# A two-layer mixer on one core: the identity and small constants move behind all other pools in SBUF

## The chip, the core and the metric

The kernel runs on one core of a Trainium2 chip. The metric is the device time of one execution in microseconds (us). TensorE is called PE in the profile, its weight loads PEld, VectorE DVE, ScalarE ACT, GpSimd POOL and SyncE SP.

## What is computed

Two layers of a mixer over 512 positions with 1024 features, all in float32. Each layer, cut to what matters:

```
xn = rmsnorm(x, pre_g);  proj = xn @ w_in
y_a = gated MLP of 128-position blocks (layernorm, lower-triangular w_s) * silu(z_a)
y_b = 8-head latent attention (low-rank q and kv, a shared rotary key) * silu(z_b)
y_c = 8-head attention over chunks of 64 with a learned bias * silu(z_c)
merged = sum over i of sigmoid(xn @ w_gate_i + gate_b_i) * (y_i @ w_branch_i)
x = x + rmsnorm(merged @ w_out, post_g)
```

## The kernel before

Each float32 matmul is done in three. An operand is split into a high part in `float32r` and a low part, the rest (`x - high`, also in `float32r`), and `mm3` adds high x high, high x low and low x high (lines 113, 114, 115) into one PSUM tile. In `t_.matmul(out, lhsT, rhs)`, `rhs` is the moving operand, which streams through the array column by column, and `lhsT` the stationary one, which is loaded ahead of it. In a row of the profile the moving operand stands first: `pm<-A_h,whi` moves `A_h` past `whi`.

Weights come in pieces of 128 x 1024 (4096 bytes in each of the 128 partitions) by DMA into `wraw`, of which there are three buffers. ACT casts a piece to `whi`, and DVE or POOL subtracts to get `wlo` (lines 102 and 107). Of `whi` and `wlo` there are four buffers each. Two helpers use them:

- `fm_unit` (features by positions): the weights are stationary, and the normalised input, `A_h` and `A_l`, moves, 512 columns at a time, 24 matmuls in a unit. `gate_units` calls it for the 24 gate pieces of a layer and then does 12 matmuls with a branch's result moving: `ybh` and `ybl` for branch b, parts of the tile `X` for branches a and c.
- `tm_unit` (positions by features): `A_h` and `A_l` are stationary and `whi` and `wlo` move, 24 matmuls in a unit. The last unit of layer 2 is done in two halves of 256 columns.

Attention adds scores (`ps_s`, with `qa`, `qb`, `ka`, `kl`, `qr`, `krs`, all from a ring of twelve tiles called `qk`, but `krs`, which is in `bk`), transposes of the softmax (`turn_p`: 128-wide matmuls with `ident` moving, `pt<-ident,pp`) and `av` (`po`, with `PT_h` and `PT_l` moving and `vt` stationary). A list `units` and a table `RATES` of credits set by hand how the units are mixed between the 128 softmax blocks of a layer's two attentions (64 a layer). The scheduler keeps that order.

Tiles lie in SBUF in the order in which pools are opened and, in a pool, in which tiles are made; each begins at the next multiple of 32 bytes in the partition. `cst` is the first pool and begins at byte 16512, a multiple of 128. It holds `ident`, 128 float32 (512 bytes), then `mhalf`, one float32, and then the large tiles, whose sizes are all multiples of 128 bytes; behind these come `col` (172 bytes) and `gbh` (96 bytes) of each layer, and then the pools `wp` (`wraw`, `whi`, `wlo`), `wk` and `sm`. So in the built program:

| tile | first byte before | modulo 128 | first byte after | modulo 128 |
|---|---|---|---|---|
| `ident` | 16512 | 0 | 228096 | 0 |
| `A_h` | 17056 | 32 | 16512 | 0 |
| `A_l`, `mrg`, `YT`, `X`, `vt`, `PT_h`, `PT_l` | 33440 to 113824 | 32 | 32896 to 113280 | 0 |
| `wraw`, `whi`, `wlo` (first of each) | 121056, 133344, 149728 | 96 | 119936, 132224, 148608 | 0 |
| `tmp`, `zs`, `ybh`, `ybl`, `bk`, `qk`, `pp`, `yo` | 166112 to 226528 | 96 | 164992 to 225408 | 0 |
| `ss`, `rs`, `bn`, `st`, `sso` (a few elements each) | 228576 and up | 0 to 96 | 227456 and up | 0 to 96 |

Parts of these tiles that matmuls use begin at multiples of 64 columns, 256 bytes, from there.

Of the kernel before, what the change touches and what calls it, by code (L numbers as in the profile page):

```python
# [8 lines left out]
F32 = mybir.dt.float32  # L9
# [6 lines left out]
P = 128  # L16
# [3 lines left out]
KT = D // P  # L20
# [3 lines left out]
H = 8  # L24
# [16 lines left out]
def trunk_kernel(ctx, tc, x, wtm, wqd, wrv, wqk, wfm, wgate, wbr, wout,  # L41
                 cols, post_g, ln_g, ln_b, sgu_wt, rel, csnd, out):
    nc = tc.nc
    v_, s_, g_, t_ = nc.vector, nc.scalar, nc.gpsimd, nc.tensor

    cst = ctx.enter_context(tc.tile_pool(name="cst", bufs=1))
    wp = ctx.enter_context(tc.tile_pool(name="wp", bufs=4))
    wk = ctx.enter_context(tc.tile_pool(name="wk", bufs=1))
    sm = ctx.enter_context(tc.tile_pool(name="sm", bufs=4))
    psm = ctx.enter_context(tc.tile_pool(name="psm", bufs=3, space=PSUM))  # L50
    pss = ctx.enter_context(tc.tile_pool(name="pss", bufs=2, space=PSUM))
    pst = ctx.enter_context(tc.tile_pool(name="pst", bufs=2, space=PSUM))
    pso = ctx.enter_context(tc.tile_pool(name="pso", bufs=1, space=PSUM))
    dr = ctx.enter_context(tc.tile_pool(name="dr", bufs=1, space=bass.MemoryType.DRAM))

    ident = cst.tile([P, P], F32, name="ident")
    make_identity(nc, ident)
    mhalf = cst.tile([P, 1], F32, name="mhalf")
    g_.memset(mhalf, -0.5)

    A_h = cst.tile([P, KT, S], F32R, name="A_h")
    A_l = cst.tile([P, KT, S], F32R, name="A_l")
# [10 lines left out]
    PT_h = cst.tile([P, TB * PTS + P], F32R, name="PT_h")  # L73
    PT_l = cst.tile([P, TB * PTS + P], F32R, name="PT_l")
    x1 = dr.tile([S, D], F32, name="x1")


    ZB = 3 * PTS + 2 * P
# [66 lines left out]
    def bk_t(n):  # L145
        return wk.tile([P, n], F32, name="bk", tag="bk", bufs=2)
# [28 lines left out]
        return i  # L175

    def load_consts(l):
        t = cst.tile([P, 4 * KT + H + 3], F32, name=f"col_{l}")
        nc.sync.dma_start(out=t, in_=cols[l])
        c = {"pre": t[:, 0:KT], "gb": t[:, KT:4 * KT], "sb": t[:, 4 * KT:4 * KT + H], "mg": t[:, 4 * KT + H:]}  # L180
        c["gbh"] = cst.tile([P, 3 * KT], F32, name=f"gbh_{l}")
        g_.tensor_scalar(out=c["gbh"], in0=c["gb"], scalar1=0.5, scalar2=None, op0=ALU.mult)
        return c

# [401 lines left out]
    for tb in range(TB):  # L586
        for hf in range(2):
            nc.sync.dma_start(out=x_rows(tb)[:, hf, :], in_=x[tb * P:(tb + 1) * P, hf * 512:(hf + 1) * 512])
        if tb == 0:
            cl = [load_consts(0)]  # L590
            raws += [load_raw(wqd[0, j], 832) for j in range(2)]
        if tb == 1:
            raws.append(load_raw(wqd[0, 2], 832))
# [4 lines left out]
    for l in range(L):  # L598
        c = cl[l]
        qk, zc, zb, st = {}, {}, {}, {}  # L600
        ya, yc, yb = [], [], []
        if l == 0:
            dgen = mla_down(l, st, raws, first)
            del raws
            step(dgen)
            norm_x(2, c)
            norm_x(3, c)
            cl.append(load_consts(1))
        else:
            st = st1  # L610
# [44 lines left out]
        for i in range(NS + LAG + 1):  # L655
# [32 lines left out]
            while credit > 0 and units and units[0][0] <= i:  # L688
                t = next(units[0][1], None)
# [14 lines left out]
        for hf in range(2):  # L704
            t = bk_t(S)
# [117 lines left out]
```

## Time and profile before

| | |
|---|---|
| median of 3 runs | 1101.63 us (1100.35 to 1102.0) |
| the profiled execution | 1102.16 us, its span 1100.4 us |
| granted PE clock, mean | 0.997 of full speed |
| busy: PE, DVE, ACT, POOL | 1075.0, 645.7, 529.2, 234.1 us |
| matmuls | 5096 |

The span is the time from the first to the last instruction of the profiled execution; 1.8 us lie around it. Matmuls overlap, so a matmul's duration is longer than the distance from its start to that of the next one; a stream's pace is read from starts.

### The profile page before, as it was taken

The page shows a single profiled execution, that of the slowest core. Times are in us where ns is not written, and L with a number is a line of the kernel's source. Part 1 is how long each engine was busy: PE and PEld are TensorE (multiplying, and loading weights), DVE is VectorE, ACT ScalarE, POOL GpSimd, SP SyncE. Part 2 cuts the span into 40 slices and gives each one's busy share as a digit, 9 for nine tenths or more (in the row PEclk, how much of TensorE's full clock was granted, in tenths as well). Part 3 has the DMA queues.
Part 4 walks back from the last instruction along what each step waited for, and adds up shares of the span by engine and source line. Part 5 has one row for each costly group of instructions (what it writes and reads, how often), then busy time and mean ns, then how long its engine had stood idle before and what let it go on. Part 6 is the DMA issues. An engine that isn't in the chain of part 4 may idle for free.

```text
span 1100.4 us, 14199 instructions
## 1 busy us (share of the span) xinstructions
PE 1075.0 (98%) x5096; PEld 886.9 (81%) x5096; DVE 645.7 (59%) x1332; ACT 529.2 (48%) x1073; POOL 234.1 (21%) x249
## 2 busy tenths in 40 slices
PE   6999999999999999999999999999999999999997
PEld 4887878888888888888787787788888888888886
DVE  5674776666566654334577756675656665534443
ACT  6454576445454543224563644664544545432331
POOL 2310132221123231210033111331212323221000
PEclk9999999999999999999999999999999999999999
DMA  7231132223233223334342322212223232323342
GB/s 238 78 101 63 52 102 85 70 81 101 77 96 96 69 86 109 95 114 153 104 133 92 104 74 67 85 58 87 91 73 106 89 86 79 102 77 96 106 150 80
DMA packets 37703, 104.65 MB, mean 95 GB/s; under 512 B 5376, under 2 KB 6400, under 8 KB 37632
## 3 DMA queue, kind: packets, MB, share of 16 engines
q1 hardware_dynamic: 37632, 103.74, 30.3%
q8 instruction: 40, 0.66, 0.3%
q14 instruction: 31, 0.25, 0.1%
HBM read 99.53 MB, written 4.19 MB: 94 GB/s over the span
## 4 chain that ended last, share of the span: by engine, by line
PE 45%; ACT 2%; DVE 2%; issue 1%; POOL 1%; DMA 0%; POOLq 0%; DVEq 0%; ACTq 0%
PE pm L114 13%; PE pm L113 13%; PE pm L115 13%; PE pt L361 2%; PE po L379 1%; PE po L378 1%; DVE wlo L107 0%; PE ps_s L419 0%; PE ps_s L418 0%; PE ps_s L436 0%; PE ps_s L438 0%; PE ps_s L437 0%; POOL rs L136 0%; PE pt L167 0%; DMA wraw<-in_wtm_dram 0%
## 5 line engine op out<-in xcount | busy, mean ns | idle before, releaser
L102 ACT CAST whi<-wraw 128x1024 fp32r<-128x1024 f32 (+3 forms) x194 | 177.1, 914 | 263.2 <-PE pm L114 156.9
L113 PE MATMUL pm<-A_h,whi 128*128 128x512 f32 x640 | 259.9, 406 | 0.0
L114 PE MATMUL pm<-A_l,whi 128*128 128x512 f32 x640 | 252.8, 395 | 0.0
L115 PE MATMUL pm<-A_h,wlo 128*128 128x512 f32 x640 | 252.7, 395 | 0.0
L107 DVE TENSOR_TENSOR wlo<-wraw,whi 128x1024 fp32r<-128x1024 f32 (+3 forms) x130 | 152.0, 1172 | 113.2 <-ACT whi L102 109.7
L107 POOL TENSOR_TENSOR wlo<-wraw,whi 128x1024 fp32r<-128x1024 f32 (+1 forms) x64 | 116.2, 1815 | 379.7 <-ACT whi L102 311.7
L113 PE MATMUL pm<-whi,A_h 128*128 128x512 f32 (+2 forms) x456 | 177.9, 390 | 2.6 <-ACT A_h L172 2.6
L114 PE MATMUL pm<-wlo,A_h 128*128 128x512 f32 (+2 forms) x456 | 176.1, 387 | 1.1 <-DVE wlo L107 1.1
L115 PE MATMUL pm<-whi,A_l 128*128 128x512 f32 (+2 forms) x456 | 176.3, 387 | 0.4 <-DVE A_l L173 0.2
L115 PEld LDWEIGHTS pm<-A_h,wlo 128*128 128x128 f32 x640 | 120.1, 188 | 29.1
L114 PEld LDWEIGHTS pm<-A_l,whi 128*128 128x128 f32 x640 | 120.4, 188 | 25.2
L113 PEld LDWEIGHTS pm<-A_h,whi 128*128 128x128 f32 x640 | 120.2, 188 | 25.2
L113 PEld LDWEIGHTS pm<-whi,A_h 128*128 128x128 f32 x456 | 86.5, 190 | 20.2 <-ACT A_h L172 4.5
L115 PEld LDWEIGHTS pm<-whi,A_l 128*128 128x128 f32 x456 | 86.4, 189 | 17.4 <-DVE A_l L173 2.0
L114 PEld LDWEIGHTS pm<-wlo,A_h 128*128 128x128 f32 x456 | 86.5, 190 | 17.0 <-DVE wlo L107 2.2
L354 DVE TENSOR_SCALAR pp<-pp,st 128x128 f32<-128x128 f32 (+3 forms) x128 | 70.2, 549 | 3.6
L367 ACT CAST PT_h<-pt 128x128 fp32r<-128x128 f32 (+3 forms) x128 | 53.9, 423 | 32.1 <-PE pt L361 31.0
L423 DVE CUSTOM_DVE_ANT_0 pp<-ps_s,bk 128x128 f32<-128x128 f32 (+1 forms) x64 | 31.2, 487 | 60.4 <-PE ps_s L419 60.1
L368 DVE TENSOR_TENSOR PT_l<-pt,PT_h 128x128 fp32r<-128x128 f32 (+3 forms) x128 | 61.6, 481 | 6.5 <-ACT PT_h L367 6.1
L361 PE MATMUL pt<-ident,pp 128*128 128x128 f32 x320 | 55.9, 272 | 1.5 <-DVE X L212 1.5
L444 ACT ACTIVATE pp<-ps_s,st 128x128 f32<-128x128 f32 (+1 forms) x64 | 33.8, 528 | 43.4 <-DVE st L442 42.7
L426 ACT ACTIVATE pp<-pp,st 128x128 f32<-128x128 f32 (+1 forms) x64 | 36.0, 563 | 37.6 <-DVE st L425 36.9
(180 smaller groups left out, 1581.8 us busy)
## 6 DMA issues: line engine op xcount, KB each, us to landing
wraw<-in_wgate_dram SPq DMA_DIRECT2D x48, 512.0 KB, 3.6
wraw<-in_wtm_dram SPq DMA_DIRECT2D x32, 512.0 KB, 3.5
wraw<-in_wfm_dram SPq DMA_DIRECT2D x32, 512.0 KB, 3.6
wraw<-in_wbr_dram SPq DMA_DIRECT2D x48, 256.0 KB, 2.6
wraw<-in_wout_dram SPq DMA_DIRECT2D x16, 512.0 KB, 3.6
bk<-in_rel_dram SPq DMA_DIRECT2D x16, 256.0 KB, 2.7
wraw<-in_wqd_dram SPq DMA_DIRECT2D x8, 416.0 KB, 4.2
mrg<-in_x_dram SPq DMA_DIRECT2D x8, 256.0 KB, 6.9
```

Of the source, the lines that this page charges most:

```text
L102: s_.copy(out=hi[:, :cols], in_=raw[:, :cols])
L107: i = e.tensor_tensor(out=lo[:, :cols], in0=raw[:, :cols], in1=f32(hi[:, :cols]), op=ALU.subtract)
L113: t_.matmul(out=ps, lhsT=lh, rhs=rh, start=start, stop=False)
L114: t_.matmul(out=ps, lhsT=lh, rhs=rl, start=False, stop=False)
L115: t_.matmul(out=ps, lhsT=ll, rhs=rh, start=False, stop=stop)
L354: v_.tensor_scalar(out=pp[:, :n], in0=pp[:, :n], scalar1=rc, scalar2=None, op0=ALU.mult)
L361: t_.transpose(pt[:, kb * P:(kb + 1) * P], pp[:, kb * P:(kb + 1) * P], ident)
L367: s_.copy(out=dst(PT_h), in_=src)
L368: v_.tensor_tensor(out=dst(PT_l), in0=src, in1=f32(dst(PT_h)), op=ALU.subtract)
L423: v_.tensor_tensor_reduce(out=pp[:, :n], in0=ps[:, :n], in1=bias[:, S - n:S], scale=1.0, scalar=-3e38, op0=ALU.add, op1=ALU.max, accum_out=mx)
L426: s_.activation(out=pp[:, :n], in_=pp[:, :n], func=AF.Exp, bias=nm, accum_out=se)
L444: s_.activation(out=pp[:, :n], in_=ps[:, :n], func=AF.Exp, bias=nm, accum_out=se)
```

## The change

The four small kinds of tile get a pool of their own, `cs`, which is opened after the other SBUF pools and so lies behind them. `make_identity` and the `memset` of `mhalf` stand some lines further down, still ahead of all other instructions of the kernel.

```diff
     sm = ctx.enter_context(tc.tile_pool(name="sm", bufs=4))
+    cs = ctx.enter_context(tc.tile_pool(name="cs", bufs=1))
     psm = ctx.enter_context(tc.tile_pool(name="psm", bufs=3, space=PSUM))
...
-    ident = cst.tile([P, P], F32, name="ident")
-    make_identity(nc, ident)
-    mhalf = cst.tile([P, 1], F32, name="mhalf")
-    g_.memset(mhalf, -0.5)
 
     A_h = cst.tile([P, KT, S], F32R, name="A_h")
...
     x1 = dr.tile([S, D], F32, name="x1")
+    ident = cs.tile([P, P], F32, name="ident")
+    make_identity(nc, ident)
+    mhalf = cs.tile([P, 1], F32, name="mhalf")
+    g_.memset(mhalf, -0.5)
...
     def load_consts(l):
-        t = cst.tile([P, 4 * KT + H + 3], F32, name=f"col_{l}")
+        t = cs.tile([P, 4 * KT + H + 3], F32, name=f"col_{l}")
...
-        c["gbh"] = cst.tile([P, 3 * KT], F32, name=f"gbh_{l}")
+        c["gbh"] = cs.tile([P, 3 * KT], F32, name=f"gbh_{l}")
```

On every engine the instructions and their order are the same in both programs; only the numbers of buffers and lines in their names differ. As an example, POOL at the start of the program, where the moved lines issue their work (`-` before, `+` after):

```order
 L819 UNCONDITIONAL_BRANCH
 masks.py:197 MEMSET ident 128x128
-L59 MEMSET mhalf 128x1
+L75 MEMSET mhalf 128x1
 L79 MEMSET PT_h 128x128
 masks.py:199 ISA
 masks.py:199 AFFINE_SELECT ident<-ident 128x128
 L80 MEMSET PT_l 128x128
-L182 TENSOR_SCALAR gbh_103<-col_101 128x24
+L182 TENSOR_SCALAR gbh_106<-col_104 128x24
```

The `memset` of `mhalf` stands where it stood, with another line number, and `gbh` and `col` have other buffer numbers; nothing moved.

## Rows read from the trace of the kernel before

**Rows 1.** The page, its head and part 1: busy time by engine.

```profile
span 1100.4 us, 14199 instructions
...
PE 1075.0 (98%) x5096; PEld 886.9 (81%) x5096; DVE 645.7 (59%) x1332; ACT 529.2 (48%) x1073; POOL 234.1 (21%) x249
```

**Rows 2.** The page, part 2: granted clock in tenths, 40 slices.

```profile
PEclk9999999999999999999999999999999999999999
```

**Rows 3.** The page, part 4: the chain that ended last, by engine.

```profile
PE 45%; ACT 2%; DVE 2%; issue 1%; POOL 1%; DMA 0%; POOLq 0%; DVEq 0%; ACTq 0%
```

**Rows 4.** PE's waits, the three longest: us in total, times, longest.

```profile
PE pt L167 <- DVE tmp L164: 10.2, 5, 7.1
PE pm L113 <- ACT A_h L172: 2.6, 2, 2.4
PE pt L361 <- DVE X L212: 1.5, 2, 0.8
```

**Rows 5.** Groups by line and form: count, then busy us, mean ns, idle.

```profile
L113 PE MATMUL pm<-A_h,whi 128*128 128x512 f32 x640 | 259.9, 406 | 0.0
...
L113 PE MATMUL pm<-whi,A_h 128*128 128x512 f32 x376 | 149.2, 397 | 0.0
...
L113 PE MATMUL pm<-X,whi 128*128 128x512 f32 x128 | 51.2, 400 | 0.0
...
L113 PE MATMUL pm<-ybh,whi 128*128 128x512 f32 x88 | 36.1, 410 | 0.0
```

**Rows 6.** Timeline of PE, 982 to 1049.3: start us, duration us, instruction.

```profile
982.06 0.39 PE L115 MATMUL pm<-ybh,wlo 128*128 128x512 f32 x1
982.29 0.39 PE L113 MATMUL pm<-A_h,whi 128*128 128x512 f32 x1
...
1049.25 0.40 PE L115 MATMUL pm<-X,wlo 128*128 128x512 f32 x1
```

**Rows 7.** Timeline of PE, 1049.4 to 1088.4.

```profile
1049.49 0.40 PE L113 MATMUL pm<-whi,A_h 128*128 128x512 f32 x1
...
1076.32 0.50 PE L114 MATMUL pm<-wlo,A_h 128*128 128x512 f32 x1
1076.65 0.39 PE L115 MATMUL pm<-whi,A_l 128*128 128x512 f32 x1
...
1088.34 0.39 PE L115 MATMUL pm<-whi,A_l 128*128 128x512 f32 x1
```

**Rows 8.** Timeline of PE, 953.1 to 955.9.

```profile
953.12 0.40 PE L113 MATMUL pm<-ybh,whi 128*128 128x512 f32 x1
953.36 0.40 PE L114 MATMUL pm<-ybl,whi 128*128 128x512 f32 x1
...
953.82 0.39 PE L113 MATMUL pm<-ybh,whi 128*128 128x512 f32 x1
...
955.86 0.39 PE L418 MATMUL ps_s<-qb 128*128 128x512 f32 x1
```

**Rows 9.** Timeline of PE, 256 columns: 232.7 to 233.1, and 1088.5 to 1094.

```profile
232.70 0.28 PE L436 MATMUL ps_s<-ka,qa 128*128 128x256 f32 x1
...
233.06 0.38 PE L361 MATMUL pt<-ident,pp 128*128 128x128 f32 x2
...
1088.57 0.28 PE L113 MATMUL pm<-whi,A_h 128*128 128x256 f32 x1
...
1093.90 0.28 PE L115 MATMUL pm<-whi,A_l 128*128 128x256 f32 x1
```

**Rows 10.** Groups by form: ACT's cast of a transposed softmax, PSUM to SBUF.

```profile
L367 ACT CAST PT_h<-pt 128x512 fp32r<-128x512 f32 x32 | 18.7, 584 | 9.3 <-PE pt L361 9.2
...
L367 ACT CAST PT_h<-pt 128x128 fp32r<-128x128 f32 x32 | 8.5, 264 | 0.7
```

**Rows 11.** SP's waits, the longest; and the loads of gate weights, us to landing.

```profile
SPq L90 <- DVE wlo L107: 551.7, 100, 20.4
...
wraw<-in_wgate_dram SPq DMA_DIRECT2D x48, 512.0 KB, 3.6
```

## The prediction

> **What bounds the kernel now.** I read the page first. TensorE (PE) is busy for 1075.0 of the 1100.4 us span, DVE for 59% and ACT for 48% [rows 1]. [...] The chain that ended last is mostly PE, with 2% each for ACT and DVE [rows 3], and its lines are the three matmuls of `mm3`. Next come PE's own waits: the two longest groups are 10.2 and 2.6 us, and six more are at most 1.5 us each [rows 4], so under 22 us in all. The kernel is one long stream of matmuls, and its time is the number of matmuls times the distance between their starts.
>
> That distance is not the mean duration of the groups (390 to 410 ns [rows 5]), since matmuls overlap; it is read from starts. [...] In the stretch that ends layer 1's mixers, 288 matmuls start from 982.29 to 1049.25: 66.96 us over 287 spacings, 233.3 ns each [rows 6]. [...]
>
> **What the spacing depends on.** In a row's `out<-in` the moving operand stands first, the stationary one second.
> - `A_h`, `A_l` or `X` moving, `whi` or `wlo` stationary: 233.3 ns [rows 6].
> - `whi` or `wlo` moving, `A_h` or `A_l` stationary: from 1049.49 to 1076.32, 115 spacings of 233.3; after one hiccup (0.33 us), from 1076.65 to 1088.34, 51 spacings of 229.2, same names and shape [rows 7]. The streams can settle in more than one rhythm.
> - `ybh` or `ybl` moving, `whi` or `wlo` stationary: after three starts, nine spacings from 953.82 to 955.86, 226.7 ns each [rows 8].
>
> `X` and `ybh` go through the same line, with the same stationary tile and shape; what differs is where the moving tile begins. Modulo 128 bytes, `A_h`, `A_l`, `X`, `vt`, `PT_h` and `PT_l` begin at 32, and `whi`, `wlo`, `ybh`, `ybl` and the twelve `qk` tiles at 96. So the start address seems to matter, and the fastest rhythm, 226.7, is that of a pair where both operands have the same offset (96, 96). After the change every one of these tiles begins at 0: one offset for all, and one that this trace never shows for a 512-wide operand. `ident` is at 0 already, but only in 128-wide transposes.
>
> **The change, part by part.** It adds and removes no instruction, and each engine's order is the same but for names; POOL's `make_identity` and `memset` stand where they stood. What changes is addresses.
>
> *PE, 512 columns wide.* 640 x 3 with `A_h`/`A_l` moving and 128 x 3 with `X` [rows 5], and 64 with `PT_h`/`PT_l`: 2368 at offset 32. 376 x 3 and 88 x 3 [rows 5], and 104 in small groups: 1496 at offset 96. Now: 2368 at 233.3, and 1496 somewhere from 226.7 to 233.3 (I take 230, between the rhythms of [rows 7, 8]); mean 232.0 over 3864. [...] Between ends so far apart I take 226.7, the rhythm of the only long-running pair with equal offsets [rows 8]. That gives 2368 x 6.6 = 15.6 us and 1496 x 3.3 = 4.9 us. Against it: the rhythm has to be found again after each break by a score, transposing or `av` matmul. The `ybh` run took three spacings for it (953.12 to 953.82, 0.70 us against 0.68); by an estimate of 200 breaks (128 softmax blocks, whose scores and transposes often stand apart) at 4 spacings of 5 ns each, 4 us are given back. Sum: 16.5 us.
>
> *PE, narrower.* 256 columns take 113.4 ns at the end (47 spacings from 1088.57 to 1093.90) and 120 among the scores (three from 232.70 to 233.06) [rows 9]. The second pair has equal offsets (96, 96), the first different ones. So equal offsets need not be best for short runs; I take 0, with 432 x 6.6 = 2.9 us as the bound either way.
>
> *ACT and DVE.* From 128 to 512 columns ACT's cast grows from 264 to 584 ns, 0.83 ns a column [rows 10]. Whatever a read that starts elsewhere saves or costs lies under PE, which waits under 22 us for all engines, half of it for `tmp` at each layer's start [rows 4]. I take 0; for a gain the bound is those 22 us. For a loss, ACT and DVE could grow by a tenth (53 and 65 us of work) and still have a third of the span free; without that cover, `whi` and `wlo` would come late and PE would wait for them.
>
> *Loads.* A 512 KB load lands 3.6 us after its issue, while SP waits 551.7 us for DVE to give a `wraw` buffer back [rows 11]. Loads wait for buffers, not the reverse: 0 either way. If a load became late, `whi` on ACT would be late next, then PE.
>
> PE has few waits, so I let the gain through whole: 1102.16 (the profiled execution, 0.5 us above the median of the three runs) less 16.5 is 1085.7; **predicted 1086**.
>
> **The rivals.**
> 1. *Address doesn't matter to the stream at this granularity, or offset 0 has the same cost as 32 and 96.* For it: one pair shows two rhythms at one set of addresses [rows 7], so the rhythm may be a matter of phase. Against it: `ybh` and `X` differ in a start address alone, and the run turns to 233.3 at once where `A_h` takes over from `ybh` at 982.29 [rows 6]. Time: 1100 to 1104, within 0.2% of now. [...]
> [...]
> 3. *Slower: one offset for all puts every stream in the slow rhythm.* Place: the 1496 matmuls at offset 96 lose their 226.7 and 229.2. For it: 256-wide pairs with equal offsets take 120 against 113.4 [rows 9]. Against it: the best 512-wide rhythm is an equal pair. [...] It decides once the mean spacing is over 232.6, which is 0.2% of the time more than now.
>
> **How the numbers follow.** About 0.2%, 2.2 us, is what a measurement of this kernel can tell from no change. Forecast (spacings of 224 to 231, 1072 to 1097): 0.38. Rival 1: 0.22. Rival 2: 0.18. Rival 3: 0.22. Faster 0.56, same 0.22, slower 0.22. The range runs from 1045, which leaves out the far half of rival 2 (0.09), to 1109, which leaves out the part of rival 3 in which spacings go past 234 (0.07); the forecast's own range is 1072 to 1097.
>
> **What would show it.** In the profile after: the starts in the stretch of `A_h,whi` matmuls near 985 to 1045, about 226.7 apart if I am right, 233.3 by rivals 1 and 3, 220 or less by rival 2; the spacing in the last stretch of `whi,A_h` the same as in that of `ybh,whi`, if the offset decides. PE's busy time falls with its span, DVE's and ACT's do not. I am wrong if spacings fall but PE begins to wait for `whi`, `wlo` or softmax (the gain would then show as waits of PE), or if the rhythm depends on the order in which streams meet and not on addresses.

## The result: 1.5% faster, and the profile after

| | before | after |
|---|---|---|
| median | 1101.0 us (4 runs, 1100.35 to 1102.0) | 1084.49 us (4 runs, 1084.22 to 1085.1) |
| ratio, 95% interval | | 0.985 [0.9833, 0.9867] |
| the profiled execution, its span | 1102.16, 1100.4 us | 1084.56, 1082.8 us |

The page after, its head, part 1 and the granted clock of part 2, against [rows 1, 2]:

```profile
span 1082.8 us, 14199 instructions
...
PE 1057.6 (98%) x5096; PEld 885.7 (82%) x5096; DVE 645.8 (60%) x1332; ACT 529.7 (49%) x1073; POOL 234.2 (22%) x249
...
PEclk9999999999999999999999999999999999999999
```

PE is busy 17.4 us less and the span is 17.6 us shorter. Of the others only PEld moved by as much as 1.2 us; DVE and ACT are within half a microsecond of [rows 1], and there are 14199 instructions as before. Nearly the whole gain lies in PE. Its two longest waits, against [rows 4]:

```profile
PE pt L167 <- DVE tmp L164: 10.0, 5, 6.9
PE pm L113 <- ACT A_h L172: 2.2, 2, 2.1
```

Together they shrank by 0.6 us, so PE did not gain by waiting less. It gained in the distance between starts. The timeline of PE after, in the stretches that answer to [rows 6, 7] (start us, duration us, instruction):

```profile
966.96 0.39 PE L113 MATMUL pm<-A_h,whi 128*128 128x512 f32 x1
...
1032.01 0.39 PE L115 MATMUL pm<-X,wlo 128*128 128x512 f32 x1
1032.23 0.39 PE L113 MATMUL pm<-whi,A_h 128*128 128x512 f32 x1
...
1058.08 0.39 PE L113 MATMUL pm<-whi,A_h 128*128 128x512 f32 x1
...
1058.83 0.40 PE L115 MATMUL pm<-whi,A_l 128*128 128x512 f32 x1
...
1070.45 0.39 PE L115 MATMUL pm<-whi,A_l 128*128 128x512 f32 x1
1070.67 0.28 PE L113 MATMUL pm<-whi,A_h 128*128 128x256 f32 x1
...
1076.31 0.28 PE L115 MATMUL pm<-whi,A_l 128*128 128x256 f32 x1
```

The same 288 matmuls now take 65.05 us over 287 spacings, 226.7 ns each, where [rows 6] had 233.3. The next stretch, `whi` or `wlo` moving, keeps 226.7 (114 spacings from 1032.23 to 1058.08) where [rows 7] had 233.3. After the hiccup at 1058.08 come 51 spacings of 227.8: the rhythm is found again, with a few longer steps (41 of the 51 are 226 or 227 ns). One thing got worse. The 256-wide matmuls of the last unit take 120.0 ns (47 spacings from 1070.67 to 1076.31) against 113.4 in [rows 9]; that is 0.3 us in all.

### The profile page after: what moved, and what is told of

Same layout as the page of the kernel before. It is cut to its first block, busy times and chain, and to the rows that moved or that the text cites. A ratio compares the mean times of both kernels' runs of the same rounds, so it can differ in the third digit from the quotient of the medians.

```text
span 1082.8 us, 14199 instructions
## 1 busy us (share of the span) xinstructions
PE 1057.6 (98%) x5096; PEld 885.7 (82%) x5096; DVE 645.8 (60%) x1332; ACT 529.7 (49%) x1073; POOL 234.2 (22%) x249
## 4 chain that ended last, share of the span: by engine, by line
PE 43%; ACT 3%; DVE 2%; issue 1%; DMA 1%; POOL 1%; POOLq 0%; DVEq 0%; ACTq 0%
PE pm L114 12%; PE pm L113 12%; PE pm L115 12%; PE pt L361 2%; PE po L379 1%; PE po L378 1%; DMA wraw<-in_wgate_dram 0%; ACT whi L102 0%; PE ps_s L419 0%; PE ps_s L418 0%; PE ps_s L436 0%; PE ps_s L438 0%; PE ps_s L437 0%; ACT tmp L160 0%; DMA wraw<-in_sgu_wt_dram 0%
## 5 line engine op out<-in xcount | busy, mean ns | idle before, releaser
L113 PE MATMUL pm<-A_h,whi 128*128 128x512 f32 x640 | 257.0, 402 | 0.0
L115 PE MATMUL pm<-A_h,wlo 128*128 128x512 f32 x640 | 249.8, 390 | 0.0
L114 PE MATMUL pm<-A_l,whi 128*128 128x512 f32 x640 | 249.5, 390 | 0.0
L115 PEld LDWEIGHTS pm<-whi,A_l 128*128 128x128 f32 x456 | 86.1, 189 | 16.5 <-DVE A_l L173 1.9
```

The source lines that it names most:

```text
L113: t_.matmul(out=ps, lhsT=lh, rhs=rh, start=start, stop=False)
L114: t_.matmul(out=ps, lhsT=lh, rhs=rl, start=False, stop=False)
L115: t_.matmul(out=ps, lhsT=ll, rhs=rh, start=False, stop=stop)
```

## The experiments

After the result two readings were open. **Theory E**: what counts is that moving and stationary operand begin at equal offsets, modulo some period. **Rival A**: what counts is that an operand begins at a multiple of 64 or 128 bytes. The change did both at once. All padding below is a tile that nothing uses; the allocation places it, and no instruction changes.

### One offset for all, at no multiple of 64; and two offsets, all multiples of 32, 64 or 128

```diff
+    cst.tile([P, 8], F32, name="pad")       # all32: 32 bytes ahead of A_h
     A_h = cst.tile([P, KT, S], F32R, name="A_h")
...
+    cst.tile([P, n], F32, name="pad")       # w64: n = 16; w32: n = 8; w128: n = 32
     x1 = dr.tile([S, D], F32, name="x1")
```

In the last three the large tiles of `cst` (`A_h`, `A_l`, `X`, `vt`, `PT_h`, `PT_l`) stay where the change put them, and everything behind, from `wraw` on, lies 64, 32 or 128 bytes further.

> The changed kernel with 32 bytes of padding ahead of A_h, so that every large tile begins at 32 modulo 128: one offset for all, but none at a multiple of 64. Theory E (equal offsets of the moving and the stationary operand make the fast rhythm): 512-wide spacing 226.7 ns in the long stretches, time 1083 to 1087. Rival A (the absolute start has to be a multiple of 64 or 128): spacing near the 233.3 of the kernel before, time 1098 to 1106.

> The changed kernel with 64 bytes of padding behind the large tiles of cst: A_h, A_l, X, vt, PT at 0 modulo 128, wraw, whi, wlo, ybh, ybl and the qk ring at 64. It has the difference of 64 of the kernel before, and all starts at multiples of 64. Theory E: A_h,whi back at 233.3, whi,A_h at 229 or 233, ybh,whi (64 and 64) at 226.7, time 1098 to 1104. Rival A with 64 as the unit: 1083 to 1087. Rival A with 128 as the unit: A_h,whi (moving at 0) fast and whi,A_h and ybh,whi slow, 1088 to 1096.

> The changed kernel with 32 bytes of padding behind the large tiles of cst: they stay at 0 modulo 128, the weights and everything behind them are at 32. A difference of 32, which neither kernel has. Theory E: slower than the changed kernel, 1090 to 1106, with ybh,whi (both at 32) still at 226.7. Rival A: A_h,whi at 226.7 (moving at 0), whi,A_h and ybh,whi slow, 1088 to 1096.

> The changed kernel with 128 bytes of padding behind the large tiles of cst: all at 0 modulo 128 still, but moving and stationary 128 bytes apart modulo 256 in the units that take weights. Theory E with 128 as the period: 1083 to 1087. Theory E with 256 or 512 as the period: 1090 to 1106. Rival A: 1083 to 1087.

| run | offsets modulo 256: `A_h`, `X`; `whi`, `ybh` | median | ratio to before, 95% interval |
|---|---|---|---|
| before | 160; 224 | 1101.0 us | |
| the change | 128; 128 | 1084.49 us | 0.985 [0.9833, 0.9867] |
| e1_all32 | 160; 160 | 1084.69 us | 0.9847 [0.9831, 0.9864] |
| e2_w64 | 128; 192 | 1101.08 us | 0.9997 [0.9988, 1.0006] |
| e3_w32 | 128; 160 | 1103.07 us | 1.0015 [1.0003, 1.0027] |
| e4_w128 | 128; 0 | 1101.34 us | 0.9998 [0.9989, 1.0008] |

The ratios of e1 to e9, here and below, are to runs of the kernel before from the same series (medians 1101.48 us for e1 to e4, 1101.38 for e5 to e8, 1101.61 for e9).

The stretch of 288 matmuls in the timelines of e1_all32, then e4_w128 (line numbers are one higher there):

```profile
967.66 0.39 PE L114 MATMUL pm<-A_h,whi 128*128 128x512 f32 x1
...
1032.71 0.39 PE L116 MATMUL pm<-X,wlo 128*128 128x512 f32 x1
```

```profile
979.19 0.40 PE L114 MATMUL pm<-A_h,whi 128*128 128x512 f32 x1
...
1046.15 0.39 PE L116 MATMUL pm<-X,wlo 128*128 128x512 f32 x1
```

65.05 us, so 226.7 ns, with every tile 32 bytes off a multiple of 128; and 66.96 us, so 233.3 ns, with every tile at a multiple of 128. Rival A falls on both sides: alignment is not needed for the gain, and doesn't bring it. The two runs with 32 and 64 bytes between the offsets have 233.3 in that stretch too (66.97 us each).

The whole traces say the same. Take the 512-wide matmuls with `A_h`, `A_l` or `X` moving past `whi` or `wlo`, each followed by another 512-wide one, and leave out steps over 245 ns (2138 steps are left in each trace). Their mean step is 233.3 ns before, 233.3, 233.0 and 232.6 in w64, w32 and w128, and 227.7 after the change and in all32. With `whi` or `wlo` moving it is 230.2 before, 233.3 in w32 and 227.5 after the change, so w32 is even a little slower than the kernel before.

So the change's gain is all in equal offsets. In e4_w128 Rival A, and Theory E with 128 as the period, had 1083 to 1087 and were wrong; the period is longer than 128.

### Each half of the change alone

```diff
 # cols_only: before, with this and the pool cs behind sm
-        t = cst.tile([P, 4 * KT + H + 3], F32, name=f"col_{l}")
+        t = cs.tile([P, 4 * KT + H + 3], F32, name=f"col_{l}")
...
-        c["gbh"] = cst.tile([P, 3 * KT], F32, name=f"gbh_{l}")
+        c["gbh"] = cs.tile([P, 3 * KT], F32, name=f"gbh_{l}")
 # ident_only: before, with ident and mhalf in cs and these two left in cst
```

> One part of the change alone: only col and gbh go to the pool behind the others; ident and mhalf stay at the front. Every large tile then begins at 32 modulo 128, with one offset (160 modulo 512) for all. Theory E (equal offsets): the whole gain, 1083 to 1087, spacing 226.7. Rival B (what counts is the identity's place, or starts at multiples of 128): no gain, 1099 to 1104.

> The other part alone: ident and mhalf go behind, col and gbh stay at the end of cst. The tiles of cst then begin at multiples of 128, the weights and all behind them at 64 modulo 128 (192 against 128 modulo 512). Theory E: no gain, 1099 to 1104, A_h,whi at 233.3 as in the run with 64 bytes of padding. Rival B: the identity's place gives the gain, 1083 to 1087, or half of it.

Measured: cols_only 1085.71 us, ratio 0.9858 [0.9843, 0.9873]; ident_only 1101.69 us, 0.9999 [0.999, 1.0008]. Both came out as Theory E had them, and the stretch of 288 matmuls too: 65.05 us, 226.7 ns each, and 66.96 us, 233.3 ns each. The identity in the change's name has no part in the gain; the moving of `col` and `gbh`, 576 bytes that stood between the large tiles and the weights, brings all of it, within the intervals. 576 is 64 modulo 256, which is the difference of offsets of the kernel before.

### The period, and how exact

```diff
 # w256: the change, with 256 bytes between PT_l and wraw
+    cst.tile([P, 16], F32, name="pad")
     x1 = dr.tile([S, D], F32, name="x1")
...
-        t = cs.tile([P, 4 * KT + H + 3], F32, name=f"col_{l}")
+        t = (cs if l else cst).tile([P, 4 * KT + H + 3], F32, name=f"col_{l}")
 # a16: the change, with A_h and A_l 16 bytes short of the common offset
-    A_h = cst.tile([P, KT, S], F32R, name="A_h")
-    A_l = cst.tile([P, KT, S], F32R, name="A_l")
+    A = cst.tile([P, 2 * KT * S + 8], F32R, name="A")
+    A_h, A_l = (A[:, i * KT * S + 4:(i + 1) * KT * S + 4].rearrange("p (k s) -> p k s", s=S) for i in range(2))
```

> The changed kernel with col of layer 0 and 64 bytes of padding between cst and the weights: 256 bytes between the offset of A_h and that of whi, modulo 512, both still at multiples of 128. Theory E with a period of 256: 1083 to 1087, spacing 226.7. Theory E with a period of 512: 1095 to 1106, spacing 230 to 236.

> The changed kernel with A_h and A_l begun 16 bytes into one common tile, so that their offset is 16 bytes less than that of all other large tiles. Theory E with exact equality needed: A_h,whi and whi,A_h slower than 226.7 (229 to 234), X,whi and ybh,whi still at 226.7, time 1090 to 1102. Theory E with a granule of 32 bytes or more: 1083 to 1088.

Measured: w256 1085.38 us, ratio 0.9848 [0.9832, 0.9865]; a16 1099.48 us, 0.9983 [0.9973, 0.9992]. With 256 bytes between the offsets the gain is all there, with 128 (1101.34 us) none of it: of the differences tried here (16, 32, 64, 128, 256), 256 alone is as good as none, and in that sense the period is 256. The stretch of 288 matmuls in w256 takes 65.06 us, 226.7 ns each. And in a16 16 bytes were enough to lose nearly all of the gain. The timeline of a16 shows the switch inside one run without a break (`A` is the common tile of `A_h` and `A_l`; `X` has the offset of `whi`, `A` has 16 bytes less):

```profile
1002.51 0.39 PE L113 MATMUL pm<-X,whi 128*128 128x512 f32 x1
...
1005.23 0.40 PE L113 MATMUL pm<-A,whi 128*128 128x512 f32 x1
...
1010.83 0.39 PE L113 MATMUL pm<-X,whi 128*128 128x512 f32 x1
```

Twelve spacings with `X` moving take 2.72 us, 226.7 each; the 24 with `A` moving behind them take 5.60 us, 233.3 each; then `X` is back at 226.7. Line, shape and the offset of the weights are alike. The 16 bytes do not cost the same in all units. In those in which `whi` moves and `A` is stationary, so that the moving one is 16 bytes ahead, the long stretch stays fast:

```profile
1046.83 0.39 PE L113 MATMUL pm<-whi,A 128*128 128x512 f32 x1
...
1072.67 0.39 PE L113 MATMUL pm<-whi,A 128*128 128x512 f32 x1
```

114 spacings, 226.7 ns; behind the next hiccup, 51 spacings from 1073.46 to 1085.10 take 228.2. After the change, with no difference, these two had 226.7 and 227.8. So a moving operand 16 bytes short of the stationary one cost 6.7 ns a matmul in these stretches, and one 16 bytes ahead nothing to 0.4 ns. Theory E's expectation (229 to 234 for both) was half wrong here. The sign of the difference and the tile that moves change together, so these runs don't tell which of the two it is; at 32 bytes (w32) both kinds of unit are slow.

One kind of part begins at no multiple of 256 bytes from its tile's start: the second half of a 416-wide piece begins 1664 bytes in. So 96 of the 192 matmuls of 416 columns still have a difference of 128 after the change.

### Which matmul pays

```diff
 # lo64: the change, with 64 bytes between the buffers of whi and of wlo
+        if not cnt[0]:
+            wp.tile([P, 16], F32, name="pad", tag="pad", bufs=1)
         lo = wp.tile([P, 1024], F32R, name="wlo", tag="wlo", bufs=4)
```

> The changed kernel with 64 bytes of padding between whi and wlo, so that wlo, ybh, ybl and the qk ring lie 64 bytes off the offset of A_h, X, vt and whi. In a unit with A_h moving, one of three stationary operands (wlo) is then off, and it is loaded while the second matmul of the three streams and is in use while the third streams. Theory L (the stream meets the load of the next stationary operand): the spacing after the second matmul (A_l,whi) is the long one, 231 to 236, the other two near 226.7; time about a third of the way back, 1088 to 1092. Rival U (the stream meets something of the operand in use): the spacing after the third (A_h,wlo) is the long one; same time. Rival W (one off operand puts the whole run in the slow rhythm): all three at 230 or more, 1096 to 1104.

Measured: 1097.33 us, ratio 0.9965 [0.9954, 0.9976], which lies over the 1088 to 1092 of Theory L and Rival U and takes back three quarters of the gain. The timeline of lo64 in the stretch of 288 matmuls (line numbers are two higher there):

```profile
977.82 0.39 PE L115 MATMUL pm<-A_h,whi 128*128 128x512 f32 x1
...
1015.25 0.39 PE L115 MATMUL pm<-A_h,whi 128*128 128x512 f32 x1
1015.48 0.39 PE L116 MATMUL pm<-A_l,whi 128*128 128x512 f32 x1
1015.71 0.40 PE L117 MATMUL pm<-A_h,wlo 128*128 128x512 f32 x1
1015.95 0.39 PE L115 MATMUL pm<-A_h,whi 128*128 128x512 f32 x1
...
1044.14 0.40 PE L117 MATMUL pm<-X,wlo 128*128 128x512 f32 x1
```

66.32 us over 287 spacings is 231.1 ns. Sorted by their place in the triple, over the 512-wide matmuls of the whole trace with `A_h` or `A_l` moving and steps over 245 ns left out, the mean step is 229.6 ns after the first, 229.8 after the second and 233.8 after the third; after the change these are 227.8, 227.6 and 228.0. Theory L falls: the step in which `wlo` is loaded, after the second, is not the long one (229.8 ns). In the trace after the change such a load of `wlo` runs from 967.18 for 0.19 us, beside the second matmul, which begins at 967.18, and ahead of the third, which begins at 967.41. The long one, 233.8 ns, is that in which `wlo` is in use, as Rival U had it. But the other two are longer than after the change too, which Rival U didn't foresee. And where `whi` and `wlo` move, the steps are 231.2, 231.9 and 232.6 (after the change 227.3, 227.6 and 227.8), so there the step of `wlo`, the second, doesn't stand out, and Rival U is borne out in one kind of unit alone. One operand of three slows the whole run part of the way, which is Rival W's direction at a smaller size. What inside PE the two operands share stays open.

## Why the prediction was right, step by step

**The bound.** It was read from starts, not from PE's busy share, which is 98% before and after. The rate of the stream was nearly the whole story: PE's busy time fell by 17.4 of the span's 17.6 us.

**The term for 512 columns.** The forecast was 20.5 us less 4 us for breaks, 16.5; the medians differ by 16.5, the two profiled executions by 17.6. The steady spacing came out as the row it was taken from, 226.7. Summed over the two traces from each matmul's start to the next one's, the 512-wide matmuls took 16.1 us less, so 4.4 of the 20.5 us were given back where 4 had been put. The breaks account for most of that. After the change there are 162 runs of steps under 245 ns between 512-wide matmuls; the first step of a run is 232.1 ns in the mean, it takes about nine to come down to 226.7, and the excess of these nine is 3.6 us in all. The prediction had fewer steps to a break and more breaks. That the sum met the medians to a tenth is luck: the profiled executions alone differ by 1.1 us more, and the 4 us were a rough estimate.

**The reason for taking 226.7.** Of the 226.7 to 233.3 ns that [rows 6, 7, 8] show, the prediction chose it since `ybh,whi` was the long-running pair with equal offsets [rows 8]. That rested on nine spacings: its runs are short, and over the whole trace of before, steps with `ybh` or `ybl` moving (230 of them, chosen as above) have a mean of 230.0. The experiments bear that reason out, and not the multiple of 128 that the change also brought: e1_all32 has the gain without it, e4_w128 has it without the gain. The prediction said that the start address seems to matter; what mattered in these runs is a difference of two start addresses, modulo 256: the stretch of 288 matmuls took 226.7 ns each at 0 and at 256 bytes, and 233.3 at 32, 64 and 128. Its sum sorted the matmuls by the offset of the moving tile; sorted by the difference, 3432 of the 512-wide ones had unequal offsets before, and 432 equal ones.

**The narrow matmuls** were put at 0 with 2.9 us either way. The 256-wide run of the last unit did get slower (113.4 to 120.0 ns), as Rival 3 had read from [rows 9], but only 48 matmuls are in it, and the difference of offsets alone does not set the 113.4. w64 and ident_only have the same difference of 64 there, and their runs of 48, first w64's and then ident_only's, take 5.53 and 5.54 us over 47 spacings, about 117.8 ns:

```profile
1087.21 0.28 PE L114 MATMUL pm<-whi,A_h 128*128 128x256 f32 x1
...
1092.74 0.28 PE L116 MATMUL pm<-whi,A_l 128*128 128x256 f32 x1
```

```profile
1087.47 0.28 PE L113 MATMUL pm<-whi,A_h 128*128 128x256 f32 x1
...
1093.01 0.28 PE L115 MATMUL pm<-whi,A_l 128*128 128x256 f32 x1
```

From start to start, all matmuls of under 512 columns together took 1.3 us less after the change (the 256-wide ones 0.4 us more), inside the 2.9.

**ACT, DVE and the loads** were put at 0. DVE's busy time went from 645.7 to 645.8 us and ACT's from 529.2 to 529.7. SP's longest wait and the gate loads, against [rows 11]:

```profile
SPq L90 <- DVE wlo L107: 542.5, 101, 20.2
...
wraw<-in_wgate_dram SPq DMA_DIRECT2D x48, 512.0 KB, 3.6
```

A load lands in the same 3.6 us, and SP still waits for buffers.

**The rivals.** Rival 1 (address doesn't matter) is refuted by a16, in which 16 bytes turn 226.7 into 233.3 and back within one run. Rival 2 (spacings of 220 ns or less) didn't come. No run here shows such a spacing, on which its chance and the range's lower end of 1045 us stood: the shortest steady spacing of 512-wide matmuls that was read in any run is 226.7 ns, and the shortest median is 1084.49 us. Rival 3 was wrong for 512 columns: with one offset for all, the stretch of 288 matmuls took 226.7 ns each, not 233.3.

## What to carry to other kernels

Where PE is the bound, read the distance between matmul starts in a long stretch and compare it across operands; here 226.7 and 233.3 ns at the same shape, 2.9% apart, were time that no wait showed. Then look where the moving and the stationary tiles begin: in this kernel the fast rhythm, 226.7 ns, needed their starts to agree modulo 256 bytes (but for the 16 bytes that cost nothing to 0.4 ns in one kind of unit), and 576 bytes of small tiles between pools broke that. To put the small constants behind the large tiles cost DVE and ACT no more than half a microsecond of busy time here (645.7 to 645.8 and 529.2 to 529.7 us). Check the difference, not the alignment: the median was 1084.69 us with all starts 32 bytes off a multiple of 128 (e1_all32), 1101.34 us with all at multiples of 128 (e4_w128).

## What the runs showed that was not expected

- A difference of 128 bytes is as bad as one of 64: 1101.34 against 1101.08 us, with 1085.38 at 256.
- 16 bytes do not cost the same everywhere: 233.3 ns with `A` moving, 16 bytes short of `whi`; 226.7 to 228.2 with `whi` moving, 16 bytes ahead of `A`.
- At 256 columns equal offsets brought no gain in the last unit: it took 120.0 ns a matmul with them, and 113.4 to 117.8 with a difference of 64. What sets the 113.4 stays open.
- Two operands at unequal offsets can run in two steady rhythms [rows 7], and a single hiccup can change the one for the other: before and in w64, 233.3 ns became about 229 behind it, but in ident_only, with the same difference, it came back to 233.3 (51 spacings from 1075.34 to 1087.24). With equal offsets this was not seen in the long stretches: after the change, 41 of the 51 steps behind the hiccup are 226 or 227 ns again.
